# One layer step on one Trainium2 core: the middle block's W_G product moved behind the last block's W_O, the last W_G made of seven half-size products, and 1/rms spread by transpositions

## The chip, the cores and the metric

The kernel runs on one core of a Trainium2 chip. The metric is the device time of one execution in microseconds. Before the change three runs gave 2661.56, 2662.13 and 2672.45 us, median 2662.13. TensorE (PE) multiplies, VectorE (DVE) and ScalarE (ACT) work on elements, POOL and SP issue most of the transfers.

## What is computed

One layer for 2048 prompt tokens and 64 sample tokens of width 1024, in float32. Cut to what matters here:

```python
h = rms_norm(x, g_pre)
vA, bA, cA, zA, q, f, iv, zB, gA, gB = split_cols(h @ w_in)
yA = (silu(zA) * bA * causal_conv3(cA * vA, conv_w)) @ w_a_out
yB = (rms_normed_scan(q, f, iv) * silu(zB)) @ w_b_out
out = (sigmoid(gA) * yA + sigmoid(gB) * yB) @ w_o
x = x + rms_norm(out, g_post)
gate = sigmoid(rms_norm(x, g_ple) @ w_ple_gate)      # W_G
x = x + (p @ w_ple_proj) * gate                      # W_ple
```

## The kernel before

Tokens are in columns, features in the 128 partitions. The 2112 tokens are three blocks of 704 columns, and a block has two halves of 352 (`BN`, `HN`). A block goes through: gates (the products for gA and gB), path B (eight heads with their scan), path A (eight rounds), W_A, W_B, W_O, two norms, W_G; the blocks overlap at their ends.

Every product of float32 matrices is three matmuls: each operand is split into a rounded part `hi` and a rest `lo`, and hi x hi, hi x lo and lo x hi are added in a PSUM bank. `split` does that with a copy on ScalarE and a subtraction on VectorE. Splits of weights are kept in DRAM (`lows`) and loaded when a weight comes again.

There are two ways to make a 1024 x 1024 product with a block. `gemm` (L523 to L525 of the profile, in `mm3`) takes one weight row of blocks and one half at a time: 8 x 3 matmuls of 352 columns into one bank, 16 banks in all, 384 matmuls. `in_turn` (L490 to L492) uses Winograd's form of Strassen's scheme over two halves of the weights and two of the tokens: seven half-size products, each for four groups of weights, of 12 matmuls each, 336 in all, with sums of weights (S1 to S4) and of operands (T1 to T4). Of the last block's stages W_A, W_B and W_O run `in_turn`, one product after the other; the sums of these weights were made ahead by `prepare_sums`, on VectorE and ScalarE with transfers on POOL's queue, beside the first block's merge (W_A, W_B) and the middle block's path A (W_O).

A norm (`final_norm`) sums squares over all eight feature blocks, adds them over the partitions with matmuls against a column of ones (`col_rstd`, L614), takes the power -1/2 on POOL (L587), and spreads the three columns of results over the partitions again (`spread`, L598): a matmul of a broadcast column with the identity, into a PSUM tile that is then copied. `final_norm` is a generator of 20 steps per call. `spread_out` puts such steps into a list of hooks, and `gemm`, `in_turn` and the others take one hook after each group of matmuls: so the order of the work around the products is set by hand. Within an engine the instructions run in the order in which they stand.

In the middle block the norm's steps stand among the next block's first seven groups of gates; then comes its W_G (`final_gate`), then the next block's path B. In the last block the first half's norm starts in W_O, and the rest of it and the second half's norm stand among the W_ple product (`ple`, L1020 to L1022, copied out of PSUM by ScalarE at L1027) and the first half's W_G; each half is a W_G of its own, 192 matmuls, and the second half's weights are split anew.

Of the kernel before, what the change touches and what calls it, by code (L numbers as in the profile page):

```python
# [10 lines left out]
F32 = mybir.dt.float32  # L11
F32R = mybir.dt.float32r
# [70 lines left out]
def hybrid_step(  # L83
# [509 lines left out]
    def spread(cols, n):  # L593

        pb = ps_attn()
        with placed():
            for i, o in tiles_of(n):
                T.matmul(pb[:, o : o + P], cols[:, i : i + 1].to_broadcast([P, P]), ident, start=True, stop=True)  # L598
        return pb[:, :n]
# [541 lines left out]
    def final_norm(bl, segs, xo, acc, h2, kept):  # L1141
# [26 lines left out]
        for j in range(KB):  # L1168
            xj = xo[j][:, c]
            if kept is not None:  # L1170
                kept["x", j] = spill("x", j)
                G.dma_start(kept["x", j], xo[j])
            if len(h2) <= j:
                h2.append((rt(dt=F32R), rt(dt=F32R)))
            t = rt()
            V.scalar_tensor_tensor(t[:, c], xj, g_ple[:, j : j + 1], rs2[:, c], ALU.mult, ALU.mult)
            split(t[:, c], h2[j][0][:, c], h2[j][1][:, c])
            yield

    def final_gate(bl, segs, xo, h2, kept, anew=False):  # L1180
        c = slice(segs[0]["off"], segs[-1]["off"] + HN)
        for j in range(KB):
            if not bl["last"]:
                pss = gemm(W_G + j, h2, segs)
            elif j == 0:
                both = gemm_by_k([W_G, W_G + 1], h2, segs, anew)
                pss = both[0]
            else:
                pss = both[1] if j == 1 else gemm(W_G + j, h2, segs, anew)
            xj = reload(kept["x", j]) if ("x", j) in kept else xo[j]  # L1190
            pj = kept["p", j] if bl["last"] else reload(kept["p", j])
            t = rt()
            for s, ps in zip(segs, pss):
                A.activation(t[:, cols_of(s)], ps, AF.Sigmoid)  # L1194
            V.tensor_tensor(t[:, c], pj[:, c], t[:, c], ALU.mult)
            V.tensor_tensor(t[:, c], t[:, c], xj[:, c], ALU.add)
            (SP if bl["last"] and j >= KB - 2 else G).dma_start(y_fm[j * P : (j + 1) * P, segs[0]["t0"] : segs[0]["t0"] + len(segs) * HN], t[:, c])
            yield

# [120 lines left out]
    for bi, bl in enumerate(blocks):  # L1320
# [8 lines left out]
        sums_ahead = prepare_sums((W_A, W_B), True) if first else prepare_sums((W_O,), False) if bi == 1 else iter(())  # L1329
# [19 lines left out]
        else:  # L1349
# [10 lines left out]
            if not nxt:  # L1360
                stages.append(out_in_turn(mg, xo, acc))
            loads(W_A, -1)
            for idx, n in in_turn(stages, a_first):
                loads(idx, n)
                if (idx, n) == (W_B, 5) and not nxt:
                    ph = [split_rt(raw) for raw in load_p(bl, G)]
                if (idx, n) == (W_O, 4):
                    norms = [final_norm(bl, [s], xo, acc, h2, None) for s in segs]
                    spread_out((norms[0], (1, 0, 1, 1, 1, 1, 1, 1)))
            if nxt:  # L1370
                mg = parts
        if nxt:
# [6 lines left out]
            norm = final_norm(bl, segs, xo, acc, h2, kept)  # L1379
# [3 lines left out]
            run(final_gate(bl, segs, xo, h2, kept))  # L1383
        else:
            gate = [final_gate(bl, [s], xo, h2, kept, anew=s is segs[1]) for s in segs]
            spread_out((norms[0], (2, 1, 0, 0, 1, 1, 4, 4)), (norms[1], (0,) * 6 + (1, 1) + (2, 2, 2, 2, 1, 0, 1, 3, 3, 2)))
            run(ple(bl, ph, kept))
            run(gate[0])
            assert not hooks
            run(gate[1])  # L1390
# [49 lines left out]
```

## Time and profile before

| | us |
|---|---|
| median of three runs | 2662.13 |
| profiled execution, first to last instruction | 2661.4 |
| TensorE busy | 2623.0 |
| VectorE busy | 1727.0 |
| ScalarE busy | 1449.6 |
| POOL busy | 349.1 |

Of the profiled execution only the span is known; what lies around it is at most the difference to the runs, 0.2 to 0.7 us for two of them. The stages of the last block lie in it so: gates and path B to about 2184, path A to 2399.8, W_A, W_B and W_O to 2565.3, W_ple to 2587.4, W_G to 2656.7. The middle block's W_G lies from 1825.2 to 1887.1, just ahead of the last block's path B.

In the profile L12 is line 12 of the kernel. A row of a group gives line, engine, operation, tiles and shape, how often, busy time in us, mean ns of one, and the idle time before. Matmuls overlap by about half, so their busy times are not to be added up. A matmul of float32 data without the split is recorded twice.

### The profile page before, as it was taken

How to read it: one execution, taken by the hardware profiler on the slowest of the kernel's cores; microseconds unless marked ns; L12 is line 12 of the kernel's file. 1: busy time of each engine (PE TensorE's matmuls, PEld its weight loads, DVE VectorE, ACT ScalarE, POOL GpSimd, SP SyncE). 2: the span in 40 equal slices, each digit the busy share in tenths (PEclk: the TensorE clock that was granted, in tenths of full speed). 3: DMA queues.
4: the chain of work that ended last, by engine and by line, in shares of the span. 5: the costliest groups of instructions: out<-in, count | busy, mean ns of one | idle time of the engine just before them, and what ended most of it. 6: DMA issues, size and time to landing. Idle time of an engine off the chain costs nothing.

```text
span 2661.4 us, 47775 instructions
## 1 busy us (share of the span) xinstructions
PE 2623.0 (99%) x16748; PEld 2600.4 (98%) x16748; DVE 1727.0 (65%) x3341; ACT 1449.6 (54%) x2782; POOL 349.1 (13%) x649
## 2 busy tenths in 40 slices
PE   7999999999999999999999999999999999999998
PEld 7999999999999999999999999999999999999988
DVE  7788888998667545466645578443355564447857
ACT  5655655454334544566645565454566654445664
POOL 1000000100432210001112210021000000001011
PEclk9999999999999999999999999999999999999999
DMA  8677777898998988776789988599867678889975
GB/s 304 217 263 269 244 260 271 299 316 288 367 344 285 352 289 275 252 227 221 222 287 357 391 304 306 182 352 307 276 218 222 222 224 263 273 274 319 302 234 168
DMA packets 362097, 735.00 MB, mean 276 GB/s; under 512 B 44064, under 2 KB 48704, under 8 KB 361856
## 3 DMA queue, kind: packets, MB, share of 16 engines
q1 hardware_dynamic: 324864, 588.20, 65.9%
q0 software_dynamic: 36704, 143.70, 14.9%
q8 instruction: 132, 2.16, 0.3%
q14 instruction: 109, 0.89, 0.1%
q10 hardware_dynamic: 288, 0.05, 0.0%
HBM read 525.71 MB, written 206.06 MB: 275 GB/s over the span
## 4 chain that ended last, share of the span: by engine, by line
PE 88%; DMA 4%; issue 3%; DVE 3%; ACT 1%; POOL 1%; SPq 0%; DVEq 0%; ACTq 0%; POOLq 0%
PE pg L357 19%; PE pg L358 19%; PE pg L359 19%; PE pg L523 4%; PE pg L525 4%; PE pg L524 4%; PE pg L491 3%; PE pg L490 3%; PE pg L492 3%; PE pa L957 1%; PE pa L921 1%; PE pa L911 1%; PE pa L959 1%; PE pa L910 1%; DMA low<-s 1%
## 5 line engine op out<-in xcount | busy, mean ns | idle before, releaser
L357 PE MATMUL pg<-r,hi 128*128 128x352 f32 x3304 | 1095.0, 332 | 6.8 <-DVE r L403 2.7
L358 PE MATMUL pg<-r,hi 128*128 128x352 f32 x3304 | 1070.1, 324 | 0.0
L359 PE MATMUL pg<-r,lo 128*128 128x352 f32 x2356 | 763.6, 324 | 0.0
L214 ACT CAST hi<-raw 128x512 fp32r<-128x512 f32 x708 | 435.6, 619 | 573.1 <-PE pg L358 206.5
L357 PEld LDWEIGHTS pg<-r,hi 128*128 128x128 f32 x3304 | 624.3, 189 | 12.6 <-DVE r L865 4.6
L358 PEld LDWEIGHTS pg<-r,hi 128*128 128x128 f32 x3304 | 623.9, 189 | 0.0
L359 PEld LDWEIGHTS pg<-r,lo 128*128 128x128 f32 x2356 | 443.9, 188 | 0.0
L359 PE MATMUL pg<-r,s 128*128 128x352 f32 x948 | 306.9, 324 | 0.0
L523 PE MATMUL pg<-r,hi 128*128 128x352 f32 x896 | 289.4, 325 | 3.1 <-ACT r L1194 2.1
L524 PE MATMUL pg<-r,hi 128*128 128x352 f32 x896 | 289.8, 324 | 0.6 <-DVE r L184 0.6
L525 PE MATMUL pg<-r,lo 128*128 128x352 f32 x756 | 244.6, 324 | 0.4 <-DVE lo L184 0.2
L184 ACT CAST hi<-raw 128x512 fp32r<-128x512 f32 x234 | 143.4, 619 | 165.4 <-PE pg L358 48.3
L184 DVE TENSOR_TENSOR r<-r,r 128x352 fp32r<-128x352 f32 (+3 forms) x274 | 169.9, 638 | 60.7 <-ACT r L184 60.0
L184 DVE TENSOR_TENSOR lo<-raw,hi 128x512 fp32r<-128x512 f32 x234 | 159.6, 688 | 65.8 <-ACT hi L184 54.2
L184 ACT CAST r<-r 128x352 fp32r<-128x352 f32 (+3 forms) x274 | 150.4, 578 | 75.1 <-DVE r L666 18.2
L184 ACT CAST hi<-s 128x512 fp32r<-128x512 f32 x160 | 99.1, 619 | 154.8 <-PE pg L358 132.7
L491 PE MATMUL pg<-r,hi 128*128 128x352 f32 x560 | 181.8, 326 | 0.0
L359 PEld LDWEIGHTS pg<-r,s 128*128 128x128 f32 x948 | 178.9, 189 | 0.1
L490 PE MATMUL pg<-r,hi 128*128 128x352 f32 x560 | 178.4, 326 | 0.1
L523 PEld LDWEIGHTS pg<-r,hi 128*128 128x128 f32 x896 | 168.0, 188 | 5.5 <-ACT r L1194 2.4
L524 PEld LDWEIGHTS pg<-r,hi 128*128 128x128 f32 x896 | 168.6, 188 | 2.0 <-DVE r L184 1.7
L371 ACT COPY hf<-pg 128x352 f32<-128x352 f32 x354 | 156.0, 446 | 6.9 <-PE pg L359 6.3
(358 smaller groups left out, 4096.9 us busy)
## 6 DMA issues: line engine op xcount, KB each, us to landing
raw<-w_blk SPq DMA_DIRECT2D x590, 256.0 KB, 4.0
lo<-low SPq DMA_DIRECT2D x404, 256.0 KB, 3.9
raw<-S SPq DMA_DIRECT2D x392, 256.0 KB, 4.1
low<-lo SPq DMA_DIRECT2D x346, 256.0 KB, 3.8
s<-low SPq DMA_DIRECT2D x304, 256.0 KB, 3.9
S<-s SPq DMA_DIRECT2D x160, 256.0 KB, 3.3
r<-w_blk POOLq DMA_DIRECT2D x48, 256.0 KB, 7.3
S<-r POOLq DMA_DIRECT2D x48, 256.0 KB, 6.1
```

The source lines that it names most:

```text
L184: return A.copy(hi, src).ins, V.tensor_tensor(lo, src, hi.bitcast(F32), ALU.subtract).ins
L214: A.copy(hi, raw)
L357: add(hi[:, k, :], xhi, start=start and k == 0, stop=False)
L358: add(hi[:, k, :], xlo, start=False, stop=False)
L359: last[0] = add(lo[:, k, :], xhi, start=False, stop=k == KH - 1).ins
L371: copied = A.copy(got[n], ps[bank])
L490: add(hi[:, k, :], xhi, start=start and k == 0, stop=False)
L491: add(hi[:, k, :], xlo, start=False, stop=False)
L492: last[0] = add(lo[:, k, :], xhi, start=False, stop=k == KH - 1).ins
L523: T.matmul(ps, hi[:, k % 4, :], xhi[:, c], start=k == ks[0], stop=False)
L524: T.matmul(ps, hi[:, k % 4, :], xlo[:, c], start=False, stop=False)
L525: last[0] = T.matmul(ps, lo[:, k % 4, :], xhi[:, c], start=False, stop=k == ks[-1]).ins
```

## The change

1. The middle block's W_G is made in the last block, behind W_O and ahead of W_ple. Its operand, the normed rows, is no longer split there and then: each row goes to DRAM as it is made (`kept["h2", j]`), is loaded again during the last block's W_O behind its first and fourth products (`rows_again`, "paced" by a wait on the last matmul so far), and split behind the third and sixth.
2. The last block's W_G is made by `in_turn` for both halves at once, behind W_ple; `gate_in_turn` takes its results, and half of the final additions go to POOL. `prepare_sums` makes its sums in the last block's path A.
3. The norms of the last block stand in W_O and among the moved W_G. The loads of p for W_ple move from W_B to behind W_O.
4. `spread` uses a transposition in place of a matmul with the identity.

```diff
-                T.matmul(pb[:, o : o + P], cols[:, i : i + 1].to_broadcast([P, P]), ident, start=True, stop=True)
+                T.transpose(pb[:, o : o + P], cols[:, i : i + 1].to_broadcast([P, P]), ident)
...
             if len(h2) <= j:
-                h2.append((rt(dt=F32R), rt(dt=F32R)))
-            t = rt()
+                h2.append(rt() if raw else (rt(dt=F32R), rt(dt=F32R)))
+            t = h2[j] if raw else rt()
             V.scalar_tensor_tensor(t[:, c], xj, g_ple[:, j : j + 1], rs2[:, c], ALU.mult, ALU.mult)
-            split(t[:, c], h2[j][0][:, c], h2[j][1][:, c])
+            if not raw:
+                split(t[:, c], h2[j][0][:, c], h2[j][1][:, c])
+            elif kept is not None:
+                kept["h2", j] = spill("h2", j)
+                G.dma_start(kept["h2", j], t)
+                h2[j] = None
...
+    def rows_again(kept, h2):
+        for _ in range(2):
+            for j in range(len(h2), len(h2) + KH):
+                hi, lo = rt(dt=F32R), rt(dt=F32R)
+                paced(G.dma_start(lo.bitcast(F32), kept["h2", j]))
+                h2.append((hi, lo))
+            yield
+            for hi, lo in h2[-KH:]:
+                split(lo.bitcast(F32), hi, lo)
+            yield
+
+    def gate_in_turn(bl, h2, xo, kept):
+        def sink(g, c, h, x, y):
+            j = g + c * KH
+            v = whole(x, y)
+            gate = hf() if y is None else v
+            A.activation(gate, v, AF.Sigmoid)
+            V.tensor_tensor(gate, gate, half(kept["p", j], h), ALU.mult)
+            (G if c else V).tensor_tensor(gate, gate, half(xo[j], h), ALU.add)
+            o = bl["t0"] + h * HN
+            (SP if (c, h) == (0, 1) else G).dma_start(y_fm[j * P : (j + 1) * P, o : o + HN], gate)
+        return dict(idx=W_G, raw=h2, sink=sink, anew=())
...
-        sums_ahead = prepare_sums((W_A, W_B), True) if first else prepare_sums((W_O,), False) if bi == 1 else iter(())
+        sums_ahead = prepare_sums((W_A, W_B), True) if first else prepare_sums((W_O,) if nxt else (W_G,), False)
...
-                if (idx, n) == (W_B, 5) and not nxt:
-                    ph = [split_rt(raw) for raw in load_p(bl, G)]
+                if idx == W_O and n in (0, 2, 3, 5):
+                    next(again)
...
-            run(final_gate(bl, segs, xo, h2, kept))
+            if first:
+                run(final_gate(bl, segs, h2, kept))
         else:
-            gate = [final_gate(bl, [s], xo, h2, kept, anew=s is segs[1]) for s in segs]
-            spread_out((norms[0], (2, 1, 0, 0, 1, 1, 4, 4)), (norms[1], (0,) * 6 + (1, 1) + (2, 2, 2, 2, 1, 0, 1, 3, 3, 2)))
+            spread_out((norms[0], (3, 0, 1, 1, 2, 2, 2, 2)), (norms[1], (0, 1, 1, 0, 1, 1, 2, 2, 2, 1, 1, 2, 2, 2, 2)))
+            raws = load_p(bl, G)
+            for j, _ in enumerate(final_gate(blocks[bi - 1], segs, rows2, kepts[bi - 1])):
+                if j == 3:
+                    ph = [split_rt(raw) for raw in raws]
             run(ple(bl, ph, kept))
-            run(gate[0])
             assert not hooks
-            run(gate[1])
+            first_rows = [narrow(half(t, 0)) for t in h2[:KH]]
+            run(in_turn([gate_in_turn(bl, h2, xo, kept)], first_rows))
```

What stands where on the engines: TensorE at the end of the last block's W_O, before (the bank `pg` of W_O's last product, then `pa` of W_ple with the split rows of p):

```order
L490 MATMUL pg_31322<-r_31342,hi_31436 128x352
L491 MATMUL pg_31322<-r_31342,hi_31436 128x352
L492 MATMUL pg_31322<-r_31342,lo_31437 128x352
L1020 MATMUL pa_31470<-r_30606,hi_31465 128x352
L1021 MATMUL pa_31470<-r_30607,hi_31465 128x352
```

And of the change (behind W_O now the middle block's W_G, `r_30366` and `r_30367` being the split of its first row):

```order
L490 MATMUL pg_30910<-r_30930,hi_31032 128x352
L491 MATMUL pg_30910<-r_30930,hi_31032 128x352
L492 MATMUL pg_30910<-r_30930,lo_31033 128x352
L523 MATMUL pg_31075<-r_30366,hi_31065 128x352
L524 MATMUL pg_31075<-r_30367,hi_31065 128x352
```

W_ple, which stood right behind W_O, now stands 384 matmuls of `gemm` later.

ScalarE at the start of W_ple, before (L1027 copies a bank of W_ple out, L1014 rounds its weights, L632 squares for the norm):

```order
L1014 CAST hi_31577<-raw_31575 128x256
L632 ACTIVATE r_31424<-r_29248 128x352
L632 ACTIVATE r_31431<-r_29248 128x352
L632 ACTIVATE r_31453<-r_29249 128x352
L632 ACTIVATE r_31460<-r_29249 128x352
L1027 COPY r_31469<-pa_31470 128x352
L1027 COPY r_31469<-pa_31478 128x352
L1014 CAST hi_31607<-raw_31605 128x256
L632 ACTIVATE r_31490<-r_29250 128x352
L632 ACTIVATE r_31495<-r_29251 128x352
L1027 COPY r_31504<-pa_31505 128x352
```

And of the change (L1191 is the sigmoid of the middle block's W_G):

```order
L1191 ACTIVATE r_31778<-pg_31722 128x352
L1014 CAST hi_31832<-raw_31830 128x256
L1014 CAST hi_31855<-raw_31853 128x256
L1191 ACTIVATE r_31778<-pg_31749 128x352
L1027 COPY r_31790<-pa_31791 128x352
L1014 CAST hi_31878<-raw_31876 128x256
L1027 COPY r_31790<-pa_31799 128x352
L1027 COPY r_31813<-pa_31814 128x352
```

The squares are gone from among the copies; they stand ahead of the last gates of the moved W_G.

ScalarE at the end of W_ple and the start of the last W_G, of the change (L184 with 352 columns splits the first rows, L214 rounds the weights, L496 copies the first product's banks):

```order
L1027 COPY r_31928<-pa_31937 128x352
L1027 COPY r_31951<-pa_31952 128x352
L184 CAST r_31968<-r_31295 128x352
L184 CAST r_31971<-r_31297 128x352
L1027 COPY r_31951<-pa_31960 128x352
L214 CAST hi_32054<-raw_32052 128x512
L184 CAST r_31974<-r_31328 128x352
L184 CAST r_31977<-r_31330 128x352
L214 CAST hi_32078<-raw_32076 128x512
L496 COPY r_31999<-pg_31986 128x352
```

Two of the four rows that the first product takes are split ahead of the last copy of W_ple, two behind it.

28 lines of the change are left out of this document (11 added, 17 removed).

## Prediction

> **What bounds the kernel now.** I read the page first: what is busy, over the whole span.
>
> ```profile
> span 2661.4 us, 47775 instructions
> PE 2623.0 (99%) x16748; PEld 2600.4 (98%) x16748; DVE 1727.0 (65%) x3341; ACT 1449.6 (54%) x2782; POOL 349.1 (13%) x649
> ```
>
> TensorE is the bound: only 38.4 us of the span are without a matmul. Time can come from fewer matmuls, from cheaper ones, or out of those 38 us. Next I took the two stretches that the change touches, by stage: the middle block's W_G, and everything from the end of the last block's W_O to the last matmul.
>
> ```profile
> 1825.20:1887.10 61.90, 61.90 (x387) 61.90 (x387) 13.01 (x15) 17.39 (x34) 12.28 (x23) 1.00 0.82 277
> 2565.30:2656.70 91.40, 84.42 (x518) 80.95 (x516) 62.97 (x130) 47.15 (x103) 14.08 (x23) 1.00 0.60 193
> ```
>
> The first is 384 matmuls of 352 columns without a gap: 61.9/384 = 0.161 us each. The second holds 480 of them (96 of the W_ple product, 384 of W_G), worth 77.4 us, in 91.4 us: TensorE stood for 7.0 us, and the other 7.0 are small matmuls of the norms and slowed steps. The waits of TensorE from W_A on, all of which lie in this second stretch:
>
> ```profile
> PE pa L1020 <- ACT r L1027: 3.6, 3, 1.7
> PE pg L523 <- ACT r L1194: 2.1, 1, 2.1
> PE pa L598 <- POOL cols L587: 0.8, 1, 0.8
> PE pg L523 <- ACT hi L214: 0.3, 1, 0.3
> ```
>
> The largest: the W_ple product has no free bank, because ScalarE's copies (L1027) stand in its queue behind squares (L632) that wait for the last block's normed rows.
>
> ```profile
> 2567.63 1.26 ACT L632 ACTIVATE r<-r 128x352 f32<-128x352 f32 x3
> 2569.15 0.50 ACT L632 ACTIVATE r<-r 128x352 f32<-128x352 f32 x1 [0.26 <-DVE r L1163]
> 2569.55 0.79 ACT L1027 COPY r<-pa 128x352 f32<-128x352 f32 x2
> ```
>
> So the end is a chain from W_O through two norms into W_G, with too little independent matmul work beside it.
>
> **The change part by part.** *Seven products for eight.* The last W_G goes from 384 matmuls to 7 x 4 x 12 = 336. The three stages that already run so, from 2399.84 to 2565.30, show the real price:
>
> ```profile
> L491 PE MATMUL pg<-r,hi 128*128 128x352 f32 x336 | 108.9, 325 | 0.0
> L490 PE MATMUL pg<-r,hi 128*128 128x352 f32 x336 | 107.8, 326 | 0.0
> L492 PE MATMUL pg<-r,lo 128*128 128x352 f32 x220 | 71.2, 324 | 0.0
> L492 PE MATMUL pg<-r,s 128*128 128x352 f32 x116 | 37.6, 324 | 0.0
> ```
>
> 1008 matmuls in 165.5 us: 55.2 us a stage, with its slower steps, against 61.9. That is 6.7 us less. The sums S1 to S4 of W_G are made beside the last block's path A: 16 loads and 32 stores of 256 KB on POOL's queue, 12.6 MB, with 16 casts and 32 additions. That I cost at nothing, since the middle block does the same for W_O beside its own path A (first two rows; the third is from the last block's path A, without it, the fourth its W_O; after the length come the busy times of TensorE, its weight loads, VectorE, ScalarE and POOL, the clock, the share and rate of the transfers):
>
> ```profile
> 1427.00:1481.00 54.00, 54.00 (x338) 53.98 (x337) 29.92 (x59) 29.19 (x62) 15.17 (x32) 1.00 1.03 383
> 1481.00:1545.00 64.00, 64.00 (x399) 64.00 (x398) 41.64 (x82) 35.93 (x72) 13.29 (x32) 1.00 1.02 377
> ...
> 2292.00:2346.00 54.00, 54.00 (x339) 54.00 (x338) 22.04 (x36) 24.87 (x46) 0.61 (x4) 1.00 0.87 273
> ...
> 2509.00:2565.00 56.00, 56.00 (x348) 54.85 (x347) 35.48 (x78) 37.46 (x83) 5.22 (x9) 1.00 0.80 253
> ```
>
> At 380 GB/s TensorE lost nothing. Five of path A's eight rounds, some 135 us, would carry 274 x 0.135 = 37.0 MB plus 12.6: 367 GB/s.
>
> *The move.* The middle W_G's 61.9 us leave 1825 and come back behind W_O, at the same count. Around it, per row: eight stores and eight loads of 352 KB more, and the splits of its rows done later, in W_O. These are eight casts and eight subtractions of 704 columns that were done before too, so the sum over the span is nil. VectorE has 35.5 of 56 us busy in W_O (fourth row) and POOL 5, so I cost them at nothing; without that cover, eight times 0.89 us. At the old place the first head of path B now follows the gates directly; it waited for nothing there, and VectorE was at 13.0 of 61.9 us, so little was being caught up. In the new place 61.9 us of matmuls need nothing of the last block, and the norms go on beside them. The four waits above, 7.0 us, lose their cause: ScalarE's order has no square left among the copies of the W_ple product.
>
> *What is late next.* First, VectorE. Between the column sums (L614) of the two halves' second norm its order holds 10 instructions of 704 columns and 33 of 352, while TensorE has 158 rows.
>
> ```profile
> L633 DVE TENSOR_TENSOR r<-r,r 128x352 f32<-128x352 f32 x28 | 14.5, 523 | 6.3 <-ACT r L632 6.3
> L1196 DVE TENSOR_TENSOR r<-r,r 128x704 f32<-128x704 f32 x16 | 14.2, 891 | 0.4
> ```
>
> 10 x 0.891 + 33 x 0.523 = 26.2 us against 158 x 0.161 = 25.4, and it starts 0.8 us late: 1.6 us of waiting at L614. Where such instructions overlap at their ends it is nothing; where loads are late, 4 us. I take 1.5. Second, the start of the last W_G: its first four rows are split on ScalarE between the last copies of the W_ple product.
>
> ```profile
> L1027 ACT COPY r<-pa 128x352 f32<-128x352 f32 x14 | 5.9, 448 | 1.9 <-PE pa L1022 1.9
> L184 ACT CAST r<-r 128x352 fp32r<-128x352 f32 x3 | 1.5, 486 | 1.1 <-DVE r L1176 1.1
> ```
>
> From the last bank but one, a copy, a cast and the 0.52 us of VectorE make 1.5 us, of which the last bank's six matmuls cover 1.0; the third row's cast, behind one more copy and a weight's cast, is some 0.5 us late in its turn. Between 0 and 2 us; I take 0.8.
>
> *Spreads by transposition.* A spread's three matmuls are six records now; a transposition is one.
>
> ```profile
> 2581.97 0.83 PE L598 MATMUL pa<-ident,cols 128*128 128x128 f32 x6
> 2582.56 0.41 PE L1020 MATMUL pa<-r,hi 128*128 128x352 f32 x1
> ```
>
> ```profile
> 2169.26 0.60 PE L971 MATMUL pa<-ident,r 128*128 128x128 f32 x4
> 2169.61 0.41 PE L357 MATMUL pg<-r,hi 128*128 128x352 f32 x1
> ```
>
> Six records hold the next matmul up for 0.59 us; four transpositions of 128x128 for 0.35, so three for about 0.25: 0.34 us saved a spread. There are 16 behind the opening:
>
> ```profile
> L598 PE MATMUL pa<-ident,cols x96: 271/275/376, 798.9 to 2616.5; 128*128 128x128 f32 x96
> ```
>
> 96/6 = 16, three of them behind W_O; the other 13 give 4.4 us, all on TensorE's path.
>
> *The end.* The last product's result is now a sum of a bank and a kept tile (one VectorE addition, L396) before the sigmoid.
>
> ```profile
> 2656.68 0.46 ACT L1194 ACTIVATE r<-pg 128x352 f32<-128x352 f32 x1 [3.40 <-PE pg L525]
> 2657.18 0.52 DVE L1195 TENSOR_TENSOR r<-r,r 128x352 f32<-128x352 f32 x1 [2.78 <-ACT r L1194]
> 2657.74 0.53 DVE L1196 TENSOR_TENSOR r<-r,r 128x352 f32<-128x352 f32 x1
> 2658.29 0.34 SPq L1197 DMA_DIRECT2D y_fm<-r  x1
> ```
>
> One more link of 0.55 us. The eight final additions that go to POOL have 1.94 us each (twelve matmuls) less the issue of a store; the profile's POOL operations lie between these ends:
>
> ```profile
> L587 POOL TENSOR_TENSOR ms<-ms,mhalf 128x4 f32<-128x4 f32 x24 | 26.1, 1088 | 223.6 <-DVE ms L585 223.6
> L1197 POOL DMA_DIRECT2D y_fm<-r x28 | 15.2, 545 | 153.3 <-issue 72.5 <-DVE r L1196 65.9 <-ACT r L1194 7.8
> L787 POOL COPY hist_p<-r 128x2 f32<-128x2 f32 x24 | 7.0, 292 | 382.0 <-DVE r L767 382.0
> ```
>
> With 1.09 + 0.55 each they still fit, and the last of them is a product and a half ahead of the end: nothing. [...]
>
> **The sum.** Before: 61.9 + 91.4 = 153.3 us. After: 61.9 for the middle W_G, 15.5 for W_ple (96 x 0.161), 55.2 for the last W_G, three norm steps at 0.59 + 0.25 (the column sums are six records too) = 2.5, waits 1.5 + 0.8: 137.4. Saved 15.9, plus 4.4 for spreads elsewhere, less 0.55: 19.75 us. Span 2661.4 - 19.75 = 2641.65. The runs' median, 2662.13, lies 0.7 us over the profiled span, and I forecast 2642.4. Left out are up to 3.5 us of slowed steps, which the old end has (7.0 less 3 x 1.18 for the norms) and the new may keep.
>
> **The rivals.** *The norms stay the bound.* POOL's queue now carries the reloads of x and W_ple's product, x for the norms, the stores and the powers (L587) in one order; if each of the three norm steps behind W_O waits 2.2 us more than taken, the time is 2649. For it: VectorE's 26.2 us against 25.4. Against: the same steps beside W_O's last products cost no wait before.
>
> *The clock.* The granted clock fell twice after column sums for which TensorE had waited, and not in path B, which is full of transpositions:
>
> ```profile
> 900.00:960.00 60.00, 58.56 (x362) 58.30 (x362) 31.20 (x48) 35.46 (x66) 8.23 (x14) 0.97 0.96 346
> 1140.00:1200.00 60.00, 60.00 (x418) 59.80 (x417) 34.13 (x82) 34.23 (x66) 4.97 (x8) 1.00 0.72 230
> 1740.00:1800.00 60.00, 58.33 (x352) 58.07 (x351) 31.03 (x48) 33.61 (x62) 11.48 (x21) 0.94 0.95 354
> ```
>
> 0.06 x 60 = 3.6 us went in the worse of them. If transpositions there prolong it by as much again, 2646. [...]
>
> *The spreads gain nothing*, because the transposition of a broadcast column runs as two records after all: 16 x 0.34 less, 2647.9. The rows of L971 speak against it.
>
> *Slower: transfers in the last path A.* If POOL's queue and the weights together got less there than the 367 GB/s needed, TensorE would wait for weights: 49.6 MB take 135 us at 367, 153 at 325 (the gain is gone) and 165 at 300, that is 2672. It decides from 325 GB/s down; the 377 to 383 of the middle block are the evidence against.
>
> **How the numbers follow.** Forecast 0.63; norms 0.15; clock 0.07; spreads 0.06; slower 0.06; the rest, 0.03, is gain beyond the sum (no waits at all: 2640 or less). The range goes from 2637 (no waits, no slowed steps) to 2653 (norms 2649 plus 3.5 of slowed steps). About 0.5%, or 13.3 us, is what a measurement of this kernel can tell from no change: faster means below 2648.8. That holds for the forecast, most of the clock's and the spreads' cases and a third of the norms': 0.71; within 0.5%: 0.22; slower: 0.07.
>
> **What would show it.** Right: W_G lines (L523 to L525) in one stretch of 62 us behind W_O without a wait; no wait at L1020; the in-turn stage at some 55 us; L598 with 48 records for 96; path A of the last block at some 370 GB/s with TensorE full. Wrong: waits at L614 or L598 behind W_O over 3 us together, idle time in path A with DMA as releaser, or a clock below 1.00 in the last 140 us.

## The result and the profile after

The changed kernel takes 2660.18 us in the median (12 runs, 2656.28 to 2666.81); the kernel before took 2663.58 on the same chip (12 runs, 2659.96 to 2672.45). The ratio is 0.9985, interval 0.9975 to 0.9996: 3.4 us faster, where 19.75 were forecast. The direction was right; the gain is 16.4 us smaller than forecast, and the time lies 17.8 us above the forecast 2642.4 and 7 us above the upper end of its range, 2653.

The profiled execution of the changed kernel is the slowest of its twelve, 2666.81 us, with a span of 2665.0; around the span lie 1.8 us in it, and 1.6 to 2.2 in every other run that shows both. So its stages are compared one by one, and its total with nothing. First the page:

```profile
span 2665.0 us, 47847 instructions
PE 2615.9 (98%) x16646; PEld 2591.9 (97%) x16646; DVE 1755.8 (66%) x3397; ACT 1461.1 (55%) x2818; POOL 393.6 (15%) x721
```

TensorE is busy for 7 us less than before (2623.0) and the span is not shorter: its idle time grew from 38.4 to 49.1 us. Where it lies, the stages show (from the start of the moved W_G: this W_G, W_ple, the last W_G, the end; last row a part of the first; columns as in the prediction: length, busy times of TensorE, weight loads, VectorE, ScalarE and POOL, the clock, share and rate of the transfers):

```profile
2511.97:2586.87 74.90, 67.99 (x415) 67.67 (x414) 48.03 (x91) 25.34 (x55) 20.04 (x34) 0.93 0.70 240
2587.00:2602.20 15.20, 15.20 (x96) 15.01 (x94) 1.78 (x2) 10.52 (x26) 0.55 (x1) 1.00 0.81 255
2602.20:2657.45 55.25, 55.13 (x337) 53.97 (x336) 41.12 (x81) 36.35 (x80) 14.83 (x20) 1.00 0.73 248
2657.45:2665.00 7.55, 0.00 (x0) 0.00 (x0) 3.55 (x8) 0.99 (x2) 0.00 (x0) 0.77 0.25 94
2550.00:2570.00 20.00, 13.09 (x68) 12.80 (x67) 9.83 (x18) 4.81 (x11) 5.29 (x8) 0.74 0.62 213
```

W_ple and the last W_G came out as forecast: 15.2 and 55.25 us, full, for 15.5 and 55.2 + 0.8. The moved W_G takes 74.9 us where 65.9 were reckoned (61.9, the norm steps, 1.5 of waiting), and the end behind the last matmul 7.55 us where it had 4.7 and 5.3 were reckoned. The last row is the centre of the miss: of 20 us TensorE worked 13, at a clock of 0.74. There is only one wait of TensorE behind W_B (waits of TensorE from 2440 on: us, times, longest):

```profile
PE pa L614 <- DVE r L633: 6.9, 1, 6.9
```

This is the second half's second column sum, the very place for which the prediction had taken 1.5 us. Between this sum and the one before it VectorE carries out the 10 instructions of 704 columns and 33 of 352 that the prediction had counted, and is busy for 24.3 us, less than the 26.2 reckoned; but it stands for 6.0 us until loads of p land (columns as above, then VectorE's largest wait there):

```profile
2527.20:2559.84 32.64, 25.73 (x164) 25.44 (x163) 24.34 (x44) 11.95 (x27) 10.65 (x20) 0.94 0.83 290
DVE r L1192 <- DMA r<-p: 6.0, 3, 4.0
```

VectorE at the end of this stretch (start, length, line, in brackets the idle time before and what ended it):

```profile
2545.08 0.89 DVE L1192 TENSOR_TENSOR r<-r,r 128x704 f32<-128x704 f32 x1 [1.14 <-DMA r<-p]
2545.89 0.58 DVE L1176 SCALAR_TENSOR_TENSOR r<-r,vec,r 128x352 f32<-128x352 f32 x1
2546.39 0.88 DVE L1193 TENSOR_TENSOR r<-r,r 128x704 f32<-128x704 f32 x1
...
2556.50 0.89 DVE L1192 TENSOR_TENSOR r<-r,r 128x704 f32<-128x704 f32 x1 [4.01 <-DMA r<-p]
2557.31 0.52 DVE L633 TENSOR_TENSOR r<-r,r 128x352 f32<-128x352 f32 x1
2557.74 0.89 DVE L1193 TENSOR_TENSOR r<-r,r 128x704 f32<-128x704 f32 x1
2558.54 1.15 DVE L633 TENSOR_TENSOR r<-r,r 128x352 f32<-128x352 f32 x2
```

The sums of squares (L633) that the column sum needs are three short instructions. They stand behind a multiplication of the moved W_G's gate with W_ple's product (L1192), and that one waits 4.0 us for its load. Why the load is late, POOL's queue shows, which issues it:

```profile
2538.92 0.54 POOL L1194 DMA_DIRECT2D y_fm<-r  x1 [2.41 <-ACT r L1191]
2539.45 0.55 POOL L1043 DMA_DIRECT2D r<-p  x1
2539.99 2.16 POOL L1153 DMA_DIRECT2D r<-x_fm  x4
2547.85 0.54 POOL L1194 DMA_DIRECT2D y_fm<-r  x1 [5.70 <-issue]
2548.38 0.55 POOL L1043 DMA_DIRECT2D r<-x  x1
2548.92 0.55 POOL L1043 DMA_DIRECT2D r<-p  x1
```

Ahead of the load of p at 2548.92 stands a store of y (L1194), for which the queue stood 5.7 us. The profile gives "issue" as its releaser, but what it stores is the result of the addition L1193 that ends at 2547.27, and that addition came behind L1192 at 2545.08, which had itself waited 1.1 us for the load issued at 2539.45. So it is a loop: load, multiply, add, store, and only behind the store the next load. Each turn is as long as a load's way plus VectorE's queue; this one lasts 11.4 us, from the multiplication at 2545.08 to that at 2556.50, while TensorE takes 7.75 us for a row (48 x 0.161). The chain of waits has the load itself, from issue to landing:

```profile
2548.92 7.56 DMA r<-p
```

It was one of four loads of 352 KB issued in a row behind the stalled store, and in these 7.56 us the transfers were busy to a share of 0.95, at 320 GB/s: the load was issued late, and then had to share full transfers.

The clock falls to half during the wait and stays there for 10.2 us, from 2555.65 to 2565.89 (the clock records). The stretch of the wait, and from its end to the end of the half clock:

```profile
2552.93:2559.84 6.91, 0.00 (x1) 0.03 (x1) 3.09 (x5) 0.79 (x2) 0.54 (x1) 0.70 0.58 218
2559.84:2565.90 6.06, 6.06 (x22) 6.06 (x23) 1.87 (x3) 0.00 (x0) 3.62 (x5) 0.50 0.31 119
```

4.2 of the 10.2 us lie inside the wait, where there was nothing to slow down; in the 6.06 us of work at half clock a matmul of 352 columns came every 0.29 us (2561.55 to 2565.65) for 0.161 elsewhere. By an estimate from the clock, 6.06 x 0.50, that cost 3.0 us more.

The end, on VectorE and on POOL:

```profile
2654.72 1.37 DVE L1217 TENSOR_TENSOR hf<-hf,r 128x352 f32<-128x352 f32 x1
...
2659.66 0.51 DVE L396 TENSOR_TENSOR hf<-r,pg 128x352 f32<-128x352 f32 x1
...
2661.35 0.52 DVE L1217 TENSOR_TENSOR hf<-hf,r 128x352 f32<-128x352 f32 x1
```

```profile
2654.74 0.95 POOL L1217 TENSOR_TENSOR hf<-hf,r 128x352 f32<-128x352 f32 x1
```

The addition on VectorE that starts beside the one on POOL takes 1.37 us for 0.52: it stands for about the whole of POOL's. VectorE is so behind that it takes the last bank (L396) 2.2 us after TensorE's last matmul. 0.95 + 0.52 less the 0.1 by which two instructions of VectorE overlap (0.08 to 0.09 us in the rows above) is 1.37. Two additions of L511 (2648.84 and 2650.91), also with both inputs in SBUF, took 1.27 us each beside POOL's of 1.15 and 1.16, and 0.53 in the kernel whose additions are all on VectorE. An addition with one input from PSUM (L396 at 2640.04) took its usual 0.52 us inside one of POOL's (2639.81, 0.94 us). The prediction had looked only at whether POOL gets done in time.

The spreads have 48 records for 96, as forecast (times of one, least, middle and most, in ns, then the first and last start):

```profile
L598 PE MATMUL pa<-ident,cols x48: 270/272/274, 802.9 to 2567.3; 128*128 128x128 f32 x48
```

And the last path A, which ends at 2347 here, runs at 370 GB/s over its last four rounds with the sums of W_G made there, and loses 1.2 us:

```profile
2239.00:2346.50 107.50, 106.33 (x659) 105.65 (x658) 62.08 (x110) 55.07 (x107) 24.70 (x52) 1.00 1.01 370
```

These 1.2 us are two waits of 0.6 us, both for VectorE (L403 and L377) and none for a transfer.

### The profile page after: what moved, and what is told of

Read it like the earlier page. It is cut to its first block, busy times and chain, and to the rows that moved or that the text cites. A ratio compares the mean times of both kernels' runs of the same rounds, so it can differ in the third digit from the quotient of the medians.

```text
span 2665.0 us, 47847 instructions
## 1 busy us (share of the span) xinstructions
PE 2615.9 (98%) x16646; PEld 2591.9 (97%) x16646; DVE 1755.8 (66%) x3397; ACT 1461.1 (55%) x2818; POOL 393.6 (15%) x721
## 4 chain that ended last, share of the span: by engine, by line
PE 85%; DMA 5%; issue 4%; DVE 4%; ACT 1%; POOL 1%; SPq 0%; DVEq 0%; ACTq 0%; POOLq 0%
PE pg L357 19%; PE pg L359 19%; PE pg L358 19%; PE pg L490 4%; PE pg L491 4%; PE pg L492 4%; PE pg L525 3%; PE pg L524 3%; PE pg L523 3%; DMA low<-s 1%; PE pa L957 1%; PE pa L921 1%; PE pa L911 1%; PE pa L959 1%; PE pa L910 1%
## 5 line engine op out<-in xcount | busy, mean ns | idle before, releaser
L359 PE MATMUL pg<-r,lo 128*128 128x352 f32 x2356 | 763.6, 324 | 1.8 <-DMA lo<-low 1.8
L214 ACT CAST hi<-raw 128x512 fp32r<-128x512 f32 x720 | 442.8, 619 | 550.9 <-PE pg L358 194.9
L357 PEld LDWEIGHTS pg<-r,hi 128*128 128x128 f32 x3304 | 623.5, 189 | 14.6 <-issue 6.4
L358 PEld LDWEIGHTS pg<-r,hi 128*128 128x128 f32 x3304 | 624.0, 189 | 0.0
L184 DVE TENSOR_TENSOR r<-r,r 128x352 fp32r<-128x352 f32 (+3 forms) x298 | 183.3, 637 | 62.5 <-ACT r L184 61.7
L525 PE MATMUL pg<-r,lo 128*128 128x352 f32 x656 | 213.3, 325 | 0.5 <-DVE lo L184 0.2
L184 ACT CAST hi<-raw 128x512 fp32r<-128x512 f32 x218 | 133.7, 619 | 143.7 <-PE pg L358 49.7
L184 ACT CAST r<-r 128x352 fp32r<-128x352 f32 (+3 forms) x298 | 161.9, 578 | 70.8 <-DVE r L666 19.0
L184 DVE TENSOR_TENSOR lo<-raw,hi 128x512 fp32r<-128x512 f32 x218 | 148.7, 687 | 58.2 <-ACT hi L184 49.2
L184 ACT CAST hi<-s 128x512 fp32r<-128x512 f32 x160 | 99.0, 619 | 151.9 <-PE pg L358 130.7
L523 PEld LDWEIGHTS pg<-r,hi 128*128 128x128 f32 x768 | 145.7, 190 | 5.2 <-ACT r L184 3.0
L524 PEld LDWEIGHTS pg<-r,hi 128*128 128x128 f32 x768 | 145.9, 190 | 1.4 <-DVE r L184 1.4
```

Source lines behind the costliest of these rows:

```text
L184: return A.copy(hi, src).ins, V.tensor_tensor(lo, src, hi.bitcast(F32), ALU.subtract).ins
L214: A.copy(hi, raw)
L357: add(hi[:, k, :], xhi, start=start and k == 0, stop=False)
L358: add(hi[:, k, :], xlo, start=False, stop=False)
L359: last[0] = add(lo[:, k, :], xhi, start=False, stop=k == KH - 1).ins
L523: T.matmul(ps, hi[:, k % 4, :], xhi[:, c], start=k == ks[0], stop=False)
```

## The experiments

Ratios are to the kernel before on the same chip. "Behind W_O" is from the first matmul of the moved W_G on.

**Spreads by transposition alone** (the kernel before with part 4 of the change):

```diff
-                T.matmul(pb[:, o : o + P], cols[:, i : i + 1].to_broadcast([P, P]), ident, start=True, stop=True)
+                T.transpose(pb[:, o : o + P], cols[:, i : i + 1].to_broadcast([P, P]), ident)
```

> The kernel before with transpositions in the spreads and nothing else. If a spread's three records for six are on TensorE's path, 16 x 0.34 us less, 5.4 us: ratio 0.998, L598 with 54 records for 108. If the granted clock falls more often after transpositions, each window of 3.4 us at half clock takes back 1.7 us: three more and the ratio is 1.000.

Measured: 2664.64 us, ratio 0.9997 (0.9987 to 1.0007). Each spread shortened its place as forecast, three transpositions holding the next matmul up for 0.25 us where six records did for 0.59, and behind the opening its profile has one slowed step of 3.4 us (at 929; mean clock 0.998) where the kernel before had three (at 928 and 6.83 us from 1781; 0.997), so the rival of the clock did not come. Yet the time stayed. TensorE waits where before it did not, in the gates of the last block (waits from 1740 to 1775):

```profile
PE pg L359 <- DMA lo<-low: 2.0, 1, 2.0
```

What comes late is a weight, and POOL's queue shows what moved. With transpositions (L1153 loads a row of x for the norm, L738 stores gates):

```profile
1736.01 0.60 POOL L1153 DMA_DIRECT2D r<-x_fm  x1
1740.35 0.54 POOL L738 DMA_DIRECT2D g__5090_21562<-r  x1 [3.74 <-ACT r L725]
1741.02 0.54 POOL L738 DMA_DIRECT2D g__5091_21564<-r  x1
1741.56 0.54 POOL L1153 DMA_DIRECT2D r<-x_fm  x1
```

And before:

```profile
1736.00 1.14 POOL L1153 DMA_DIRECT2D r<-x_fm  x2
1740.03 0.54 POOL L738 DMA_DIRECT2D g__5090_21562<-r  x1 [2.89 <-ACT r L725]
1740.71 0.54 POOL L738 DMA_DIRECT2D g__5091_21564<-r  x1
```

The second reload of x now stands behind two stores that wait for ScalarE, and starts 5 us later. From 1740 to 1745 the transfers then ran so, with transpositions:

```profile
1740.00:1745.00 5.00, 5.00 (x34) 5.00 (x33) 4.89 (x8) 3.88 (x8) 3.23 (x6) 1.00 0.87 312
1745.00:1750.00 5.00, 5.00 (x33) 5.00 (x33) 4.12 (x7) 3.44 (x6) 1.68 (x4) 1.00 1.03 403
```

And before:

```profile
1740.00:1745.00 5.00, 5.00 (x34) 5.00 (x33) 4.60 (x8) 3.61 (x7) 2.17 (x4) 1.00 1.04 383
```

71 GB/s over 5 us is 0.36 MB, one row of x, left for a stretch that is full at 400 GB/s. In the gates at 905 TensorE waits for a weight too, 1.0 us, and there too a reload of x has slipped behind stores by 5 us (887.3 for 882.4). Both waits together are 3.0 of the 5.4 us that the spreads should give. That is a reading of the trace, and this one execution was 3.3 us shorter than the profiled one of the kernel before, so it doesn't by itself show why the median stayed; the last runs test the reading.

**Reloads two rows ahead** (the changed kernel; the moved W_G asks for its rows of x and p two rows before it needs them):

```diff
-            xj, pj = reload(kept["x", j]), reload(kept["p", j])
+            fetch(j + 1)
+            xj, pj = got[j]
...
+            fetch(j + ahead)
```

> The changed kernel, but in the moved W_G the loads of x and of the W_ple rows are asked for two rows ahead of use. Theory A (a loop in POOL's queue: the load of one row stands behind the store of an earlier one, which waits for VectorE, which waits for the load before): the 6.9 us wait of TensorE at L614 goes, and with it the half clock behind it (10.2 us at half, 5.1 lost): about 12 us less than the changed kernel, ratio to before 0.994, the W_G stretch 63 us for 74.9. Theory B (VectorE simply has too much work ahead of that column sum): no change, the wait stays within 2 us of 6.9.

Measured: 2653.94 us, ratio 0.9965 (0.9952 to 0.9978). That is 5 to 6 us less than the changed kernel (by the ratios, by the medians) where theory A had 12, but not the "no change" of theory B. VectorE waits for no load of p any more, TensorE's wait is down to a fifth, and the clock is at half for 3.4 us instead of 10.2; the moved W_G takes 68.9 us.

```profile
PE pa L614 <- DVE r L633: 1.5, 2, 1.3
```

**The column sum later** (the changed kernel; the second half's steps are put so that its second sum comes 96 matmuls later, reloads as they were):

```diff
-            spread_out((norms[0], (3, 0, 1, 1, 2, 2, 2, 2)), (norms[1], (0, 1, 1, 0, 1, 1, 2, 2, 2, 1, 1, 2, 2, 2, 2)))
+            spread_out((norms[0], (3, 0, 1, 1, 2, 2, 2, 2)), (norms[1], (0, 1, 1, 0, 1, 1, 1, 1, 1, 1, 1, 1, 0, 1, 1, 0) + (1,) * 8))
```

> The changed kernel with the second half's second column sum 96 matmuls (15.5 us) later in the moved W_G, the loads left where they were. Theory B: the wait at L614 goes, W_G 63 us, ratio to before 0.994. Theory A: the loop in POOL's queue goes on, some 9 us a row against TensorE's 7.75, so VectorE is still late there: a wait of 3 us or more and a stretch at half clock, ratio 0.996 to 0.999.

Measured: 2647.07 us, ratio 0.9938 (0.9927 to 0.995). This is theory B's number: no wait is left behind W_O, nor a slowed step before the last matmul, and the moved W_G takes 65.0 us.

```profile
2535.00:2555.00 20.00, 20.00 (x127) 20.00 (x126) 13.97 (x22) 7.65 (x17) 6.47 (x12) 1.00 0.90 313
```

VectorE still waits for p in this profile (2.8 us, 1.85 of them at 2536), and no longer hurts anyone. So the late loads alone are not the cause, nor is the plan alone: the sum stood too early for an order of VectorE that holds load-fed work ahead of it. Of the 9.9 us between the two lengths of the moved W_G (74.9 and 65.0) the reloads ahead alone take 6.0.

**All final additions on VectorE** (the changed kernel):

```diff
-            (G if c else V).tensor_tensor(gate, gate, half(xo[j], h), ALU.add)
+            V.tensor_tensor(gate, gate, half(xo[j], h), ALU.add)
```

> The changed kernel with all the final additions of the last W_G on VectorE, none on POOL. If POOL's additions slow VectorE (L1217 took 1.37 us beside one, 0.52 alone), the way from the last matmul to the end of the span is 5.3 us for 7.6, so 2 us less than the changed kernel. If VectorE is merely full there, eight more additions of 0.52 us make the end later by 1 to 4 us.

Measured: 2656.40 us, ratio 0.9975 (0.9964 to 0.9986). The end behind the last matmul falls from 7.6 to 5.8 us in the profiles, as the first theory has it; the wait at L614 is 5.3 us in this one. By the ratios it is 0.0010 faster than the changed kernel, and the intervals overlap.

**Later sum and additions on VectorE** (both edits above):

> The changed kernel with the second column sum of the second half's norm 96 matmuls later and all final additions on VectorE. Theory A (the two faults add up: the 6.9 us of waiting with the half clock behind it, and the backlog that POOL's additions make at the end): TensorE ends as with the later sum alone (2637.6 in its profile), the end behind it falls from 7.7 to about 5.8 us, so about 2 us less than 2647.1: 2645, ratio 0.993. Rival B (VectorE, which now has eight more additions of 0.52 us beside the last W_G, falls behind the banks): no better than 2647, with waits of TensorE for a free bank at the in-turn lines.

Measured: 2650.68 us, ratio 0.9954 (0.9942 to 0.9967): worse than expected, and not better than the later sum alone. Rival B is not the reason, since TensorE waits for nothing behind W_O. There are waits for weights in the last block's gates again:

```profile
PE pg L359 <- DMA lo<-low: 1.7, 1, 1.7
PE pg L359 <- DMA s<-low: 1.3, 1, 1.3
```

But they don't explain it: with 0.8 us in the first gates they make 3.8 us, and the later sum alone has 3.5. Its profiled span is 4.6 us longer, and 4.7 us of difference arise in the middle block (from the last column sum of the first block's norm to the first of the middle block's, 929.33 to 1737.91, for 928.86 to 1732.78), in waits for VectorE and a slowed step, far from both edits. The intervals overlap; what the loss is, or whether there is one, stays open.

**And the reloads two rows ahead as well:**

> The same with the reloads of x and of W_ple's product asked two rows ahead as well. If the later sum already takes all that the late loads cost TensorE (theory A), this adds nothing: 2645, ratio 0.993, within 1 us of the kernel without it. Rival B (the queue's loop of load, addition, store and next load still holds VectorE up and shows somewhere as a wait of TensorE): 1 to 3 us less, 2642 to 2644.

Measured: 2648.06 us, ratio 0.9942 (0.9929 to 0.9954); the intervals overlap by half. The 1 to 3 us of rival B can't be told from this. TensorE waits no more than 0.2 us behind W_O in either profile, so I put nothing down to the reloads.

**The same without transpositions** (later sum, additions on VectorE, spreads as matmuls):

> The kernel with the later sum and the additions on VectorE, but with the spreads as matmuls with the identity again (six records each). Theory A (the gain of a transposition is given back as waits for weights where the gates' transfers run at 400 GB/s, and only spreads elsewhere pay: three of the 16 behind the opening lie behind W_O, 1.0 us): 0 to 1.5 us slower than with transpositions, 2645 to 2647. Rival B (the transpositions pay 0.34 us each everywhere, and the kernel before with transpositions alone missed it by chance): 5.4 us slower, 2650.

Measured: 2649.20 us, ratio 0.9949 (0.9936 to 0.9963), against 0.9954 with transpositions. Again they are worth nothing, and again the profile with matmuls has no wait for a weight in the gates.

**The move without the seven products** (the changed kernel, the last W_G as two halves of 192 matmuls, no sums of W_G):

```diff
-            first_rows = [narrow(half(t, 0)) for t in h2[:KH]]
-            run(in_turn([gate_in_turn(bl, h2, xo, kept)], first_rows))
+            h3 = [split_rt(t) for t in h2]
+            run(half_gate(bl, [segs[0]], xo, h3, kept))
+            run(half_gate(bl, [segs[1]], xo, h3, kept))
```

> The changed kernel with the last W_G as in the kernel before: two halves by the ordinary product, 384 matmuls in place of 336, no sums of W_G made in path A. The move, the norms' places and the transpositions stay. Theory A (the seven products pay their 6.7 us in full, and cost nothing in path A): 6.7 us slower than the changed kernel by the last W_G (61.9 for 55.2 us), less some 2 us at the end, where POOL's additions no longer lie: 2660.2 + 4.7 = 2665, ratio 1.000. Rival B (making the sums of W_G in path A costs transfers and VectorE something that TensorE pays there): 2662 or less. The wait at L614 behind W_O stays at 5 to 7 us in both.

Measured: 2664.51 us, ratio 1.0006 (0.9997 to 1.0015), as theory A has it: the seven products pay. The wait at L614 stays, 6.3 us. The price of the sums is small; without them the same rounds of path A run full at 278 GB/s, where the changed kernel had 370 and lost 1.2 us:

```profile
2231.45:2338.95 107.50, 107.50 (x670) 107.50 (x669) 49.03 (x85) 51.21 (x96) 3.75 (x12) 1.00 0.88 278
```

**Five rows of x ahead for the middle norms** (later sum, additions on VectorE, transpositions; the reload that had slipped behind the stores is issued early):

```diff
-        for _ in range(2 if bl["last"] else 4):
+        for _ in range(2 if bl["last"] else 5):
```

> The kernel with the later sum, the additions on VectorE and transposed spreads, in which the middle norms ask for five rows of x ahead instead of four. In the kernels with transposed spreads POOL's queue has the second later reload of x (L1153) behind two stores of gates (L738) that wait for ScalarE, and 5 us later than with matmuls; the transfers have room then (312 GB/s at 1740) and run full at 400 GB/s from 1745 on, where TensorE waits for weights. Theory A (this shift gives the spreads' gain back): no waits of TensorE for lo and s at 905 and 1760 any more, 3 to 5 us less than the kernel with four rows ahead: 2646 to 2648, ratio 0.9935 to 0.994. Rival B (the gates are bound by the sum of their transfers, wherever the reloads stand): the waits at 905 and 1760 stay at 2 to 3 us each, time 2650, ratio 0.9954 as it was.

Measured: 2643.52 us, ratio 0.9927 (0.9915 to 0.994), 7 us less by the ratios than with four rows, and the intervals don't overlap. That is more than the 3 to 5 us expected, and than the 3.8 us of waits for weights that are gone; the rest is not explained. No wait for a weight is left in the gates, and the transfers are full at 1740 again:

```profile
1740.00:1745.00 5.00, 5.00 (x33) 5.00 (x33) 5.00 (x8) 3.47 (x8) 2.68 (x5) 1.00 1.03 377
```

**The same with the eight additions on POOL:**

> The same with the eight final additions on POOL, as in the changed kernel: it tells the price of POOL's additions on one chip. Theory A (they slow VectorE's additions beside them and leave a backlog of some 2 us at the end): 2 us slower than with the additions on VectorE, and 7.7 us between TensorE's last matmul and the end for 5.8. Rival B (the end is the same within 1 us, since eight more additions load VectorE instead): no difference.

Measured: 2648.03 us, ratio 0.9943 (0.9931 to 0.9955): 4.5 us slower by the medians. The profiles show 1.4 us of it, an end of 7.5 us for 6.1. Between the later sum alone (0.9938, on POOL) and with VectorE's additions (0.9954) the difference went the other way, on two chips. So the price at the end, 1.4 to 1.8 us in every pair of profiles, is shown; in the times it is at the edge of what they tell.

**All four mends:**

> All four mends together: the later sum, the reloads of x and of W_ple's product two rows ahead, the additions on VectorE, the middle norms' reloads five ahead. If the predicted sum was right but for these places, it comes to the forecast's 2642 (ratio 0.9925 to the before of the same chip); if something else is lost, it stays at 2646 or above.

Measured: 2646.18 us, ratio 0.9939 (0.9928 to 0.9951); its profiled span, 2641.5 us, is the shortest of all. The median stands where the expectation had "something else is lost", not at the forecast's 2642; the interval overlaps that of the kernel without the reloads ahead, which add nothing that shows.

**The seven products without the move** (the kernel before with the last W_G in turn for both halves, the middle W_G at its old place, transpositions):

```diff
-            gate = [final_gate(bl, [s], xo, h2, kept, anew=s is segs[1]) for s in segs]
+            spread_out((norms[0], (2, 1, 0, 0, 1, 1, 4, 4)), (norms[1], (0,) * 6 + (1, 1) + (6, 6, 4, 2)))
...
-            run(gate[0])
-            run(gate[1])
+            first_rows = [narrow(half(t, 0)) for t in h2[:KH]]
+            run(in_turn([gate_in_turn(bl, h2, xo, kept)], first_rows))
```

> The kernel before with only the last W_G made in turn behind W_ple (336 matmuls for 384, its sums made in path A, the additions half on POOL) and the transposed spreads; the middle block's W_G stays at its old place, and both halves' norms must be done among W_ple and the last W_G's start. Theory A (the seven products need the moved W_G as cover: the whole norm of both halves now stands in front of the in-turn product, with only W_ple's 15.5 us beside it): TensorE waits 25 us or more between W_O and the last W_G, so 15 to 30 us slower than before, ratio 1.006 to 1.012. Rival B (the norms' chain hides as it did before): 6.7 us faster, ratio 0.9975.

Measured: 2668.76 us, ratio 1.0025 (1.0015 to 1.0035), 6.6 us slower: between the two theories. The norms find less cover than before, but not as little as I had expected (waits of TensorE from 2480 on):

```profile
PE pg L490 <- ACT r L184: 3.7, 4, 2.0
PE pa L1020 <- ACT r L1027: 3.6, 3, 1.7
PE pa L614 <- DVE r L633: 3.1, 1, 3.1
PE pa L598 <- POOL cols L587: 1.2, 1, 1.2
PE pg L491 <- DVE r L184: 0.6, 2, 0.4
```

12.2 us of waits stand where the kernel before had 7.0, and beside them the clock is at half for 10.2 us (0.91 from 2603 to 2659). From the end of W_O to the last matmul it takes 91.7 us, before 91.4: what 48 fewer matmuls save is waited away. The end behind it takes 8.1 us for 4.7; the rest of the 6.6 us I can't place. So neither part paid alone as it was run here. With this plan the seven products need the move as cover for the norms. The other way round it is not shown: the kernel with the move alone still had the early column sum in it, whose mend was worth 0.0047 to the changed kernel, and it was not run with that mend.

**Two controls for the fifth row.** The mended kernel with matmuls for its spreads and five rows ahead:

> The kernel with the later sum, the additions on VectorE and five rows of x ahead, with the spreads as matmuls again. Theory A (the fifth row only undoes the late reload that transpositions brought, where TensorE waited for weights; with matmuls it never waited there): it adds nothing to the kernel with matmuls and four rows ahead, ratio 0.9945 to 0.9955, and so stands 4 to 6 us above the one with transpositions and five rows (0.9927). Rival B (the fifth row pays by itself, transpositions never do): 0.9925 to 0.993, as with transpositions.

Measured: 2646.40 us, ratio 0.9941 (0.9928 to 0.9954). And the kernel before with transpositions and five rows, nothing else:

> The kernel before with transposed spreads and five rows of x ahead, nothing else. Theory A: the waits of TensorE for lo and s at 906 and 1758 are gone and the spreads' 5.4 us show: ratio 0.998 (0.9975 to 0.9985). Rival B (spreads are worth nothing, or the fifth row pays only with the moved W_G): 0.9995 to 1.0005, as with four rows.

Measured: 2659.02 us, ratio 0.9985 (0.9976 to 0.9994), with no wait for a weight at 906 or 1758. With five rows transpositions are worth 0.0014 to 0.0015 of the time in both kernels (0.9941 to 0.9927, and 1 to 0.9985), some 4 us; with four rows they were worth nothing in both (0.9949 to 0.9954, and 1 to 0.9997). That is theory A, though 0.9941 lies just under the 0.9945 to 0.9955 that it had. The traces hold no exception: in all nine profiles with transpositions and four rows TensorE waits in the gates for weights, 2.5 to 4.1 us, and in none of the three with matmuls or the four with five rows. With matmuls the fifth row moved the ratio by 0.0008, inside its interval, so a part of its own is not excluded; and of these differences only that of the last kernel to the kernel before is clear of its interval.

## Why the prediction was wrong

The direction and most of the mechanism were right; three terms of the sum were not: the wait at the column sum, the spreads, and POOL's additions. The prediction's own sign of being wrong came, over 3 us of waiting at L614. The steps in their order, with what the profile of the changed kernel and the runs made of them.

- **Seven products for eight, 6.7 us**: right. 55.25 us in the profile, and the kernel without them 0.0021 slower, some 5.6 us; what their longer end costs is already taken off in this.
- **Sums of W_G in path A, nothing**: nearly. The transfers ran at 370 GB/s, for 367 reckoned, and TensorE waited 1.2 us, for VectorE. The slower rival, which needed less than 325 GB/s, did not come.
- **The four old waits of 7.0 us go**: right. W_ple has none and takes 15.2 us.
- **Start of the last W_G, 0.8 us**: nothing was lost there.
- **"Where such instructions overlap at their ends it is nothing; where loads are late, 4 us. I take 1.5."** This is the step that failed. The wait was 6.9 us, 5.4 more than taken, and 6.06 us of work at half clock cost, by the estimate from the clock, another 3.0, for which the sum had no term (it left slowed steps out); the moved W_G took 9.0 us more than reckoned. The mechanism had been named, for the rival that the norms stay the bound spoke of POOL's queue with "the reloads of x and W_ple's product, x for the norms, the stores and the powers (L587) in one order". But the sum counted VectorE's busy time only, 26.2 us against 25.4, as if each operand were there. The busy time was no more than that, 24.3 us; 6.0 us of standing for p and 0.8 for x came on top. The long instructions among them need rows that POOL's queue loads behind a store that waits for VectorE; the slack of such a ring can't be read off busy times. The later sum (no wait, 65.0 us) and the reloads ahead (1.5 us, 68.9) both show it.
- **Spreads, 0.34 us each, "the other 13 give 4.4 us, all on TensorE's path"**: the size of one was right, the path was not. In the gates TensorE has no slack in its weights: the transfers run at 400 GB/s, and a reload that slipped by 5 us took back what the spreads gave (3.3 us of waits for weights in the profile of the changed kernel, in the gates of the two later blocks). With the reload early they give about 4 us.
- **POOL's eight additions, "nothing"**: 2.3 us at the end beyond the 0.55 of the added link. 1.8 of them went when VectorE made these additions: VectorE had stood while POOL added, and it was behind. The other 0.5 us stay open.
- **0.7 us between span and median**: 1.6 to 2.2 us lie between the span and the time of an execution in all runs that show both, so this was about 1 us too little.

From W_O's end to the last matmul 153.3 us became 145.5, a gain of 7.8 where 15.9 were reckoned (two stages stand in the first number, as in the prediction's sum). So 8.1 us are missing there, 2.3 at the end, 3.3 in the gates and 1.2 in path A: 14.9 of the 16.4 us by which the gain fell short of the forecast.

The two profiled spans can't confirm the gain: that of the changed kernel is 3.6 us longer. At the last column sum of the middle block's norm (1780.81 us before, 1789.49 after) it is 8.7 us behind, and 4.3 of these already at the first column sum behind the opening (879.03 and 883.37); the slowed steps in the opening alone differ from profile to profile (one of 3.41 us before, three here). One wait of 1.2 us in the middle block's W_O at 1666, for ScalarE's split, lies between nothing and 1.2 us from profile to profile, and a slowed step follows it here (3.41 us from 1668.19).

With three of the places mended (sum later, additions on VectorE, reload early) the stretch behind W_O takes 135.5 us to the last matmul, for the forecast's 137.4, and the kernel 0.9927 of the time before, for a forecast of 2642.4 / 2662.13 = 0.9926. That the total meets so well is partly luck: the stretch is 1.9 us shorter than the sum, the end 0.8 longer (6.08 for 5.28), and the kernel with the reloads ahead as well, which should be no worse, stands at 0.9939. So the sum was about right for a kernel with those three mends, not for the one that was to be forecast.

## What to carry to other kernels

Where VectorE's order holds work that waits for a load, and the queue that issues the load holds a store of that work's result ahead of it, reckon the loop's turn (issue to landing, plus the work, plus the issue of the store; 11.4 us here), not the busy time, and put whatever TensorE needs ahead of such work or well behind it. A cut in TensorE's time pays only where its weights come early enough (the spreads gave nothing while TensorE waited 2.5 to 4.1 us in the gates for weights, and some 4 us without these waits): look at the transfers' share in each stage in which it lies, and at whether the cut shifts a large transfer into a full stretch. Work moved to an engine that stands still is free only if it doesn't hold up the engine beside it (here VectorE, 1.37 us for 0.52 beside POOL's 0.95).

## What the runs showed of the hardware

- The wait of 6.9 us cost more than its length, by the estimate from the clock 3.0 us: beside it the clock was at half for 10.24 us, 4.2 of them inside the wait. Beside a wait of 5.3 us it was at half for 6.8 us (additions on VectorE; 0.83 from 2535 to 2555), beside one of 1.3 us for 3.4 (reloads two rows ahead; 0.91 from 2535 to 2555). The half clock lasted 3.41, 6.83 and 10.24 us in the profiles of the kernel before and of the changed kernel, the end of the span aside. Not each wait had such a step: the four of the kernel before behind W_O, 7.0 us with one of 2.1, had none (clock 1.00 from 2565.30 to 2656.70).
- Additions of 352 columns with both inputs in SBUF did not run side by side on VectorE and POOL in the end of the changed kernel: 1.37 us on VectorE (2654.72) beside 0.95 on POOL, for 0.52 alone, and twice 1.27 beside 1.15 and 1.16.
- Over stretches of 5 us laid end to end the transfers reached 419 GB/s at most, in the profile of the kernel before (705 to 710) and in that of the changed kernel (1820 to 1825); over stretches of 60 us 387 and 385 (1440 to 1500). In a stretch at some 400 GB/s a single row of 0.36 MB that came 5 us later was seen as 1.2 us (changed kernel) to 2.0 us (transpositions alone) of waiting at TensorE for one weight.
- A load of 352 KB took 7.56 us from issue to landing, with the transfers busy to 0.95: it was one of four issued within 2.2 us behind a store for which the queue had stood 5.7 us.
